# A hybrid decoder trunk on one core: six memory-key chunks opened at once, and each gated head's small products in one TensorE burst

## The chip, the cores and the metric

The kernel runs on one core of one Trainium2 chip. Its time is that of one execution on the device, in microseconds (us). Several runs are made and their median is taken. A profiled execution on the same kind of chip gives the trace from which all rows below are read; its span is counted from the first to the last instruction.

## What is computed

One decoder layer with 256 tokens and a width of 2048, all in float32, with 256 memory tokens beside it. In short:

```
memn = rms_norm(mem);  u = rms_norm(x)
proj = u @ w_in
h = x + [sigmoid(g_hg) * (hgrn2(q, f, i, og) @ w_bhg)
         + sigmoid(g_m2) * (mamba2(z, xbc, dt) @ w_bm2)] @ w_out
k, v = split(memn @ wkv)                       # 16 key chunks of 128 columns
h = h + softmax(rms_norm(h) @ wq . k) v @ wo
h = h + (gelu(conv(gate)) * up) @ w_down       # gate, up = rms_norm(h) @ w_up
out = rms_norm(h)
```

The gated branch (hgrn2) has 16 heads of 128 keys and 128 values. For each head, S_t = diag(f_t) S_{t-1} + k_t v_t^T and o_t = S_t^T q_t; then o is gated, normed over its 128 values and weighted.

## The kernel before

Activations lie transposed, features on the 128 partitions and the 256 tokens along the free axis. Each activation is held as two halves side by side, the rounded high part and the rest (512 columns, names s1 and s2), and each weight likewise as two tiles, hi and lo. A projection of one 128-column chunk is 16 products hi x [high, rest] of 512 columns (L158) followed by 16 products lo x high of 256 columns (L160), all into one bank of the pool proj. Weights arrive in float32 (1 MB a chunk, tile raw, SP's queue); ScalarE casts hi (L103) and VectorE subtracts for lo (L104), each in two pieces of 1024 columns. There are five buffers each of hi and lo, which is two and a half chunks, and the loads run two chunks ahead (AHEAD). Value projections (L188 to L190) work on tokens and take four 1 MB loads of 24 products each.

The first stage makes the 16 chunks of memory keys from s1. It opens with three chunks in step over pieces of two and then four k-blocks (L276 to L289), so that work starts before a whole chunk is there. It also makes the sums of squares of mem and x, the norms from products with ones (row_rsqrt, col_rsqrt), and s2 from x.

In the second stage three projections are made for each head, and four value loads ahead of each fourth head. The scan of a head is a Python generator, hg_scan. A list named background holds the running generators, and step(), called ahead of every weight chunk, advances each by one yield. A head's parts are: the decays (L389 to L428), the weighted decays (L430 to L437), the small products of the levels 1 to 16 into a bank of the pool lev (L445 to L455) and their masking into sm, the 32- and 64-wide blocks and the product across the two halves of the tokens into a bank of the pool misc (L466 to L476), the copies into the matrix a, the weighing of the values by a (L489, L490), and the norm (L499 and what follows). Each part comes one chunk after the one ahead of it. In the end the tile framework's scheduler decides the order on every engine, and may put one part's products among another's. Mamba's scan and the attention run as generators in the same way.

Of the kernel before, what the change touches and what calls it, by code (L numbers as in the profile page):

```python
# [19 lines left out]
P = 128  # L20
# [23 lines left out]
B = 32  # L44
MASKW = SMALL * B
# [4 lines left out]
def hybrid_trunk(ctx, tc, xT, memT, par, cst, msk, w_ka, w_va, w_hg, w_hv, w_ghg, w_bhg, w_dt,  # L50
# [102 lines left out]
    def hl_run(ps, parts, first, last):  # L153


        n = len(parts) - 1
        for i, (wh, _, hl) in enumerate(parts):
            PE.matmul(ps, lhsT=wh, rhs=hl, start=first and i == 0, stop=False)  # L158
        for i, (_, wl, hl) in enumerate(parts):
            PE.matmul(ps[:, 0:T], lhsT=wl, rhs=hl[:, 0:T], start=False, stop=last and i == n)  # L160
# [4 lines left out]
    def mm_three(ps, w, j, hl, first, last):  # L165
        wh, wl = w(j, P)
        PE.matmul(ps[:, 0:T], lhsT=wh, rhs=hl[:, 0:T], start=first, stop=False)
        PE.matmul(ps[:, 0:T], lhsT=wh, rhs=hl[:, T:2 * T], start=False, stop=False)
        PE.matmul(ps[:, 0:T], lhsT=wl, rhs=hl[:, 0:T], start=False, stop=last)
# [7 lines left out]
    def project_tok(hl):  # L177

        ps = [pj.tile([P, 512], F32, name="proj") for _ in range(2)]
        for i in range(4):  # L180
            w = weights()
            for j in range(4):
                k = 4 * i + j
                wh, wl = w(j, 512)
                for g in range(2):
                    x1 = hl[:, k, g * P:(g + 1) * P]
                    x2 = hl[:, k, T + g * P:T + (g + 1) * P]
                    PE.matmul(ps[g], lhsT=x1, rhs=wh, start=(k == 0), stop=False)  # L188
                    PE.matmul(ps[g], lhsT=x1, rhs=wl, start=False, stop=False)  # L189
                    PE.matmul(ps[g], lhsT=x2, rhs=wh, start=False, stop=(k == KD - 1))  # L190
# [75 lines left out]
    with tc.tile_pool(name="st", bufs=1) as st:  # L266
# [8 lines left out]
        nc.sync.dma_start(out=par_t[:, 0:8 * KD], in_=par[:, 0:8 * KD])  # L275
        first = [fetch(st, "raw0", 3) for _ in range(3)]  # L276
        pss = [pj.tile([P, 512], F32, name="proj") for _ in first]
        for k0, k1 in ((0, 2), (2, 4), (4, 8), (8, 12), (12, 16)):
            nc.sync.dma_start(out=mraw[:, k0:k1, :], in_=memT[:, k0:k1, :])
            for src, w in first:  # L280
                nc.sync.dma_start(out=w[0][:, P * k0:P * k1], in_=src[:, P * k0:P * k1])
            for k in range(k0, k1):
                split_scaled(s1[:, k, :], mraw[:, k, :], pc("mem_g", k))
            for (_, w), ps in zip(first, pss):
                halves(w, P * k0, P * k1)
                mm_run(ps, viewer(w[2]), [(k, s1[:, k, :]) for k in range(k0, k1)], k0 == 0,
                       k1 == KD)
            for k in range(k0, k1):
                sumsq(st, macc, mraw[:, k, :], k == 0)  # L289
        state["used"] = len(first)  # L290
        prefetch(AHEAD)

        for n in range(KD):
# [4 lines left out]
            if 3 <= n < 7:  # L298
                k = 4 * n - 12
                nc.sync.dma_start(out=xraw[:, k:k + 4, :], in_=xT[:, k:k + 4, :])  # L300
            if n == 7:
# [84 lines left out]
    def hg_scan(h, kq, zz, v):  # L386
# [18 lines left out]
        so = mp.tile([P, T], F32, name="so", bufs=2)  # L405
# [32 lines left out]
        yield True  # L438
# [507 lines left out]
```

## Time and profile before

| | us |
|---|---|
| median of 3 runs (range) | 2309.02 (2308.66 to 2310.59) |
| the profiled execution | 2308.46 |
| its span | 2306.6 |
| TensorE busy | 2285.2 (99%) |
| VectorE busy | 1579.5 (68%) |
| ScalarE busy | 1363.1 (59%) |

The busy time of an engine is a mean over stages that have different limits. A busy TensorE is not a TensorE at its peak: ends of products are modelled, so what a stretch costs is read from the starts of successive products. The granted clock is 0.999 of full speed over the span.

### The profile page before, as it was taken

To read this page: it belongs to the slowest core of one execution; us is meant where nothing else is said; L and a number is where in the kernel's file an instruction comes from. 1 tells how busy PE (TensorE), PEld (TensorE's weight loads), DVE (VectorE), ACT (ScalarE), POOL (GpSimd) and SP (SyncE) were. 2 spreads that over 40 slices of the span, in tenths; PEclk is the share of its full clock that TensorE was granted. 3 is DMA by queue.
4 is the path that set the end of the run, shared out by engine and by line. 5 is a ranking of instruction groups with operands and counts; after the bars stand their busy time and mean duration, and the time that the engine had idled before them with its cause. 6 is when DMAs were issued, how large, how long until landed. Compare 5 with 4: busy or idle time off the path is not lost.

```text
span 2306.6 us, 35693 instructions
## 1 busy us (share of the span) xinstructions
PE 2285.2 (99%) x14210; PEld 1993.5 (86%) x14210; DVE 1579.5 (68%) x2652; ACT 1363.1 (59%) x2126; POOL 1.3 (0%) x9
## 2 busy tenths in 40 slices
PE   8999999999999999999999999999999999999998
PEld 7888888888888888888888888888888888888887
DVE  8768778797555777765576765667777767755554
ACT  7566667677445778774465654556555555544443
POOL 0000000000000000000000000000000000000000
PEclk9999999999999999999999999999999999999999
DMA  8644444445555555445565644565555555556554
GB/s 288 246 171 162 158 159 163 165 161 197 183 188 187 190 192 184 173 165 192 186 242 207 224 158 171 176 217 196 184 195 188 185 196 186 187 173 198 197 196 142
DMA packets 74951, 433.92 MB, mean 188 GB/s; under 512 B 8320, under 2 KB 15904, under 8 KB 31008
## 3 DMA queue, kind: packets, MB, share of 16 engines
q1 hardware_dynamic: 74208, 430.72, 53.6%
q8 instruction: 111, 1.82, 0.3%
q10 hardware_dynamic: 576, 0.92, 0.1%
q14 instruction: 56, 0.46, 0.1%
HBM read 425.28 MB, written 6.32 MB: 187 GB/s over the span
## 4 chain that ended last, share of the span: by engine, by line
PE 94%; DVE 4%; ACT 1%; DMA 1%; issue 0%; SPq 0%; DVEq 0%
PE proj L158 54%; PE proj L160 28%; PE proj L188 3%; PE proj L189 3%; PE proj L190 3%; DVE lo L104 1%; DVE e L421 1%; PE misc L158 1%; DMA mraw<-in_memT 1%; PE lev L454 0%; DVE e L434 0%; PE misc L607 0%; PE misc L473 0%; PE misc L160 0%; PE misc L476 0%
## 5 line engine op out<-in xcount | busy, mean ns | idle before, releaser
L158 PE MATMUL proj<-s,hi 128*128 128x512 f32 x5248 | 1276.2, 393 | 8.4 <-ACT hi L103 5.7
L104 DVE TENSOR_TENSOR lo<-raw,hi 128x1024 fp32r<-128x1024 f32 (+4 forms) x827 | 937.0, 1158 | 468.3 <-PE proj L160 379.1
L158 PEld LDWEIGHTS proj<-s,hi 128*128 128x128 f32 x5248 | 962.6, 188 | 198.0 <-ACT hi L103 7.8
L103 ACT CAST hi<-raw 128x1024 fp32r<-128x1024 f32 (+4 forms) x827 | 821.6, 997 | 515.0 <-PE proj L158 410.2
L160 PEld LDWEIGHTS proj<-s,lo 128*128 128x128 f32 x5248 | 678.4, 191 | 28.2 <-DVE lo L104 0.3
L160 PE MATMUL proj<-s,lo 128*128 128x256 f32 x5248 | 688.6, 283 | 0.0
L195 ACT COPY jt<-proj 128x256 f32<-128x256 f32 x265 | 97.9, 370 | 168.5 <-PE proj L160 168.0
L188 PE MATMUL proj<-hi,s 128*128 128x512 f32 x256 | 101.0, 394 | 0.0
L190 PE MATMUL proj<-hi,s 128*128 128x512 f32 x256 | 99.8, 390 | 0.0
L189 PE MATMUL proj<-lo,s 128*128 128x512 f32 x256 | 99.7, 389 | 0.0
L789 DVE SCALAR_TENSOR_TENSOR gc<-g,par_t,gc 128x255 f32<-128x255 f32 x88 | 42.6, 484 | 54.7 <-ACT gc L787 53.1
L158 PE MATMUL proj<-ha,hi 128*128 128x512 f32 x300 | 73.7, 392 | 0.0
L158 PEld LDWEIGHTS proj<-ha,hi 128*128 128x128 f32 x300 | 54.4, 189 | 10.1
L559 DVE SCALAR_TENSOR_TENSOR sz<-t,par_t,sz 128x255 f32<-128x255 f32 (+2 forms) x96 | 46.2, 481 | 19.8 <-ACT sz L556 18.3
L190 PEld LDWEIGHTS proj<-hi,s 128*128 128x128 f32 x256 | 48.0, 188 | 10.2
L188 PEld LDWEIGHTS proj<-hi,s 128*128 128x128 f32 x256 | 48.1, 188 | 9.4
L189 PEld LDWEIGHTS proj<-lo,s 128*128 128x128 f32 x256 | 48.1, 188 | 9.3
L201 ACT COPY jt<-proj 128x256 f32<-128x256 f32 x47 | 17.5, 372 | 64.4 <-DVE h L200 46.5
L160 PEld LDWEIGHTS proj<-ha,lo 128*128 128x128 f32 x300 | 39.9, 191 | 2.3
L206 DVE SCALAR_TENSOR_TENSOR s<-h,par_t,s 128x256 fp32r<-128x256 f32 x32 | 15.5, 485 | 36.8 <-ACT s L205 36.6
L160 PE MATMUL proj<-ha,lo 128*128 128x256 f32 x300 | 40.7, 282 | 0.0
L636 ACT ACTIVATE gs<-r 128x256 f32<-128x256 f32 x32 | 13.4, 418 | 39.7 <-DVE r L196 39.7
(257 smaller groups left out, 1525.9 us busy)
## 6 DMA issues: line engine op xcount, KB each, us to landing
raw<-in_w_up SPq DMA_DIRECT2D x88, 1024.0 KB, 4.8
raw<-in_w_hg SPq DMA_DIRECT2D x48, 1024.0 KB, 4.8
raw<-in_w_m SPq DMA_DIRECT2D x48, 1024.0 KB, 4.8
raw<-in_w_dn SPq DMA_DIRECT2D x64, 704.0 KB, 4.1
raw<-in_w_hv SPq DMA_DIRECT2D x16, 1024.0 KB, 4.9
raw<-in_w_ghg SPq DMA_DIRECT2D x16, 1024.0 KB, 4.8
raw<-in_w_bhg SPq DMA_DIRECT2D x16, 1024.0 KB, 4.8
raw<-in_w_gm SPq DMA_DIRECT2D x16, 1024.0 KB, 4.8
```

The source lines that it names most:

```text
L103: S.copy(out=hi[:, c - a:d - a], in_=raw[:, c:d])
L104: V.tensor_tensor(out=lo[:, c - a:d - a], in0=raw[:, c:d], in1=hi[:, c - a:d - a].bitcast(F32), op=ALU.subtract)
L158: PE.matmul(ps, lhsT=wh, rhs=hl, start=first and i == 0, stop=False)
L160: PE.matmul(ps[:, 0:T], lhsT=wl, rhs=hl[:, 0:T], start=False, stop=last and i == n)
L188: PE.matmul(ps[g], lhsT=x1, rhs=wh, start=(k == 0), stop=False)
L189: PE.matmul(ps[g], lhsT=x1, rhs=wl, start=False, stop=False)
L190: PE.matmul(ps[g], lhsT=x2, rhs=wh, start=False, stop=(k == KD - 1))
L195: S.copy(out=tmp, in_=ps[:, T:2 * T])
L201: S.copy(out=tmp, in_=ps[:, T:2 * T])
L421: V.tensor_tensor(out=lev[hw].rearrange("p (n c i) -> p n c i", c=2, i=hw), in0=free(bb, 0, [(2 * hw, nb), (T + hw, 2), (1, hw)]), in1=fre ...
L559: V.scalar_tensor_tensor(out=o[:, s:T], in0=raw[:, 0:T - s], scalar=pc("m2_cw", 4 * c + 3 - s), in1=o[:, s:T], op0=ALU.mult, op1=ALU.add)
L789: V.scalar_tensor_tensor(out=gc[:, s:T], in0=g[:, 0:T - s], scalar=pc("f_cw", 3 * c + 2 - s), in1=gc[:, s:T], op0=ALU.mult, op1=ALU.add)
```

## The change

Three things are changed.

First, the opening. Six chunks (NS) are made at once, from a new array w_k0 in which the six chunks' columns of two k-blocks lie together. Each k-block of 768 columns is cast into one hi and one lo tile and used for all six chunks, which sum into the four banks of proj and the two of lev; the last four k-blocks are done chunk by chunk. The gains (par_t) load on ScalarE's queue, ahead of its table load, and eight products of ones with ones stand first on TensorE. The load of x, its squares and the making of s2 move to other chunks.

Second, a head's small products. The levels, the 32- and 64-wide blocks and the product across the halves are written in one part. The product across the halves has a bank of its own (ep), the wide blocks share the levels' bank, and the second 64-wide block goes to partitions 64 to 127. The next two parts come three chunks later each (pause, gap), so that in one call of step() head h-2's norm, head h-1's weighing and head h's blocks follow each other.

Third, products issued inside step() are kept in program order (mm, PIN). Everywhere else PE.matmul is only replaced by mm, which is the same instruction.

```diff
+    def mm(*args, **kwargs):
+        ins = PE.matmul(*args, **kwargs)
+        if PIN:
+            tc.keep_in_program_order(ins)
...
-    order = [w_ka[n] for n in range(KD)]
+    order = [w_ka[n] for n in range(KD - NS)]
...
     def step():
+        PIN.append(1)
         for gen in list(background):
             if next(gen, False) is False:
                 background.remove(gen)
+        PIN.pop()
...
+    def pause(n):
+        for _ in range(n):
+            yield True
...
-        nc.sync.dma_start(out=par_t[:, 0:8 * KD], in_=par[:, 0:8 * KD])
-        first = [fetch(st, "raw0", 3) for _ in range(3)]
-        pss = [pj.tile([P, 512], F32, name="proj") for _ in first]
-        for k0, k1 in ((0, 2), (2, 4), (4, 8), (8, 12), (12, 16)):
...
+        nc.scalar.dma_start(out=par_t[:, 0:8 * KD], in_=par[:, 0:8 * KD])
+        nc.scalar.preload_act_table_set("natural_log_exp_and_others")
+        wps = pm_.tile([P, 512], F32, name="misc")
+        for _ in range(8):
+            mm(wps[:, 0:P], lhsT=ones, rhs=ones, start=True, stop=True)
+        pss = [pj.tile([P, 512], F32, name="proj") for _ in range(4)] \
+            + [pl.tile([P, 512], F32, name="lev") for _ in range(NS - 4)]
+        W = NS * P
+
+        def first_block(k, raw):
+
+            split_scaled(s1[:, k, :], mraw[:, k, :], pc("mem_g", k))
+            hi = wp.tile([P, 1024], F32R, name="hi", bufs=WB)
+            lo = wp.tile([P, 1024], F32R, name="lo", bufs=WB)
+            for c, d in ((0, W // 2), (W // 2, W)) if k < 2 else ((0, W),):
+                S.copy(out=hi[:, c:d], in_=raw[:, c:d])
+                V.tensor_tensor(out=lo[:, c:d], in0=raw[:, c:d], in1=hi[:, c:d].bitcast(F32),
+                                op=ALU.subtract)
+            sumsq(st, macc, mraw[:, k, :], k == 0)
+            return hi, lo
...
+        for kk in range(KD // 2):
+            raw = st.tile([P, 2 * W], F32, name="raw0", bufs=4)
+            if kk == 0:
+                for k in range(2):
+                    nc.sync.dma_start(out=mraw[:, k, :], in_=memT[:, k, :])
+                    nc.sync.dma_start(out=raw[:, k * W:(k + 1) * W],
+                                      in_=w_k0[kk, :, k * W:(k + 1) * W])
+            else:
+                nc.sync.dma_start(out=mraw[:, 2 * kk:2 * kk + 2, :], in_=memT[:, 2 * kk:2 * kk + 2, :])
+                nc.sync.dma_start(out=raw, in_=w_k0[kk])
+            for i in range(2):
+                k = 2 * kk + i
+                parts[k] = first_block(k, raw[:, i * W:(i + 1) * W])
+                if k < KD - 4:
+                    cols = [column(n, k) for n in range(NS)]
+                    for n, (wh, _, hl) in enumerate(cols):
+                        mm(pss[n], lhsT=wh, rhs=hl, start=k == 0, stop=False)
+                    for n, (_, wl, hl) in enumerate(cols):
+                        mm(pss[n][:, 0:T], lhsT=wl, rhs=hl[:, 0:T], start=False, stop=False)
+        for n in range(NS):
+            hl_run(pss[n], [column(n, k) for k in range(KD - 4, KD)], False, True)
...
-            if 7 <= n < 15:
-                for k in (2 * n - 14, 2 * n - 13):
+            if n >= 10:
+                for k in range((n - 10) * KD // 6, (n - 9) * KD // 6):
...
-        so = mp.tile([P, T], F32, name="so", bufs=2)
+        so = mp.tile([P, T], F32, name="ho", bufs=4)
...
-        yield True
+        yield from pause(2)
...
+        ep = pl.tile([P, 512], F32, name="lev")
         W1 = B + B // 2
+        o32 = 2 * W1 + 2 * (SMALL - 1) * B
+        o64 = o32 + 2 * B
+        mm(ep[:, 0:P], lhsT=ec[:, 0:P], rhs=ec[:, P:T], start=True, stop=True)
+        for g in range(2):
+            t0 = g * P
+            mm(lp[g * 2 * B:(g + 1) * 2 * B, o64:o64 + 2 * B],
+                      lhsT=lev[64][:, t0:t0 + 2 * B], rhs=lev[64][:, t0 + 2 * B:t0 + 4 * B],
+                      start=True, stop=True)
+        for g in range(2):
+            for s0 in (0, 2 * B):
+                t0 = g * P + s0
+                mm(lp[s0:s0 + B, o32 + g * B:o32 + (g + 1) * B], lhsT=lev[32][:, t0:t0 + B],
+                          rhs=lev[32][:, t0 + B:t0 + 2 * B], start=True, stop=True)
...
+        S.copy(out=a[:, P:2 * P], in_=ep[:, 0:P])
...
-        yield True
-        ps = pm_.tile([P, 512], F32, name="misc")
+        for s0 in (0, 2 * B):
+            rows = slice(s0, s0 + B)
+            V.tensor_copy(out=free(a[rows, :], s0 + B, [(2 * P, 2), (1, B)]),
+                          in_=lp[rows, o32:o64].rearrange("p (g t) -> p g t", g=2))
         for g in range(2):
...
+            V.tensor_copy(out=a[0:2 * B, 2 * g * P + 2 * B:2 * g * P + 4 * B],
+                          in_=lp[g * 2 * B:(g + 1) * 2 * B, o64:o64 + 2 * B])
...
-        yield True
+        gap = 3 if h + 1 < HEADS else 2
+        yield from pause(gap)
...
-        yield True
+        yield from pause(gap)
```

The order of instructions shows three places. The first is the start of TensorE's program. Before, with numbers of buffers (proj_105 to proj_107 are the banks of the three chunks, hi and lo their weights):

```order
L158 MATMUL proj_105<-s1_76,hi_116 128x512 x2
L160 MATMUL proj_105<-s1_76,lo_117 128x256 x2
L158 MATMUL proj_106<-s1_76,hi_124 128x512 x2
L160 MATMUL proj_106<-s1_76,lo_125 128x256 x2
L158 MATMUL proj_107<-s1_76,hi_132 128x512 x2
L160 MATMUL proj_107<-s1_76,lo_133 128x256 x2
```

And now, where every product of TensorE has the line of mm, L66:

```order
L66 MATMUL misc_102<-ones_80 128x128 x8
L66 MATMUL proj_111<-s1_75,hi_124 128x512
L66 MATMUL proj_112<-s1_75,hi_124 128x512
L66 MATMUL proj_113<-s1_75,hi_124 128x512
L66 MATMUL proj_114<-s1_75,hi_124 128x512
L66 MATMUL lev_115<-s1_75,hi_124 128x512
L66 MATMUL lev_116<-s1_75,hi_124 128x512
L66 MATMUL proj_111<-s1_75,lo_125 128x256
```

Eight products of ones stand first, and one cast pair (hi_124, lo_125) serves six banks where three pairs served three.

The second place is a head on TensorE, in the middle of the second stage. Before (e holds the decays of the levels, ec those across the halves, a the assembled matrix, vc the values, sqs the squares for the norm):

```order
L470 MATMUL misc<-e_1727 32x32 x2
L473 MATMUL misc<-e_1727 64x64
L476 MATMUL misc<-ec 128x128
L158 MATMUL proj<-s_77,hi 128x512 x16
L160 MATMUL proj<-s_77,lo 128x256 x16
L489 MATMUL misc<-a_1170,vc 128x256
L490 MATMUL misc<-a_1170,vc 128x128
L158 MATMUL proj<-s_77,hi 128x512 x16
L160 MATMUL proj<-s_77,lo 128x256 x16
L499 MATMUL misc<-sqs,ones_r 128x256
L448 MATMUL lev<-ql,kq 32x48 x4
L454 MATMUL lev<-e_1990 32x32 x5
```

And now:

```order
L66 MATMUL proj<-s_76,lo 128x256 x16
L66 MATMUL misc<-sqs,ones_r 128x256 x2
L66 MATMUL misc<-a_1178,vc 128x256
L66 MATMUL misc<-a_1178,vc 128x128
L66 MATMUL lev<-ec 128x128
L66 MATMUL lev<-e_1992 64x64 x2
L66 MATMUL lev<-e_1992 32x32 x4
L66 MATMUL lev<-ql,kq 32x48 x4
L66 MATMUL lev<-e_1991 32x32 x12
L66 MATMUL lev<-e_1992 32x32 x4
L66 MATMUL lev<-ql,kq 32x48 x4
L66 MATMUL lev<-e_1991 32x32 x12
```

Where a group of small products stood after each projection, all of them now stand after the third.

The third place is VectorE just behind those products (sm and a take the masked blocks, lf, bb and e belong to the next head, lo is the weights' cast). Before:

```order
L463 COPY_PREDICATED sm<-msk_t,lev 128x64 x4
L479 COPY a_1170<-sm 32x2x32 x4
L104 TENSOR_TENSOR lo<-raw,hi 128x1024 x2
L196 TENSOR_TENSOR sz<-proj,jt 128x256
L482 COPY a_1170<-misc 32x2x32 x2
L484 COPY a_1170<-misc 64x2x64
L395 TENSOR_TENSOR lf<-lf,w 128x256
L402 SCALAR_TENSOR_TENSOR t<-sz,w 128x256
L396 TENSOR_TENSOR lf<-lf,w 128x256
L406 SCALAR_TENSOR_TENSOR so<-sz,w 128x256
L398 SCALAR_TENSOR_TENSOR bb<-cst_t,lf 128x256
L104 TENSOR_TENSOR lo<-raw,hi 128x1024
```

And now:

```order
L225 TENSOR_TENSOR sqs<-sq,sqs 128x256
L526 COPY_PREDICATED sm<-msk_t,lev 128x64 x2
L530 COPY a_1177<-lev 32x2x32 x2
L533 COPY a_1177<-lev 64x64 x2
L537 COPY a_1177<-sm 32x2x32 x4
L441 TENSOR_TENSOR lf<-lf,w 128x256
L448 SCALAR_TENSOR_TENSOR t<-sz,w 128x256
L442 TENSOR_TENSOR lf<-lf,w 128x256
L452 SCALAR_TENSOR_TENSOR ho<-sz,w 128x256
L444 SCALAR_TENSOR_TENSOR bb<-cst_t,lf 128x256
L112 TENSOR_TENSOR lo<-raw,hi 128x1024
L467 TENSOR_TENSOR e_2256<-bb 128x256 x3
```

Three casts stood between the masking and the decays' differences; one stands there now, behind all copies and the scan.

## Rows read from the trace of the kernel before

**Rows 1.** The page's chain that ended last, by line, share of the span

```profile
PE proj L158 54%; PE proj L160 28%; PE proj L188 3%; PE proj L189 3%; PE proj L190 3%; DVE lo L104 1%; DVE e L421 1%; PE misc L158 1%; DMA mraw<-in_memT 1%; PE lev L454 0%; DVE e L434 0%; PE misc L607 0%; PE misc L473 0%; PE misc L160 0%; PE misc L476 0%
```

**Rows 2.** Timeline, TensorE, K stage: start us, us, engine, line, operation, count

```profile
39.61 3.82 PE L158 MATMUL proj<-s,hi 128*128 128x512 f32 x16
...
45.18 3.82 PE L158 MATMUL proj<-s,hi 128*128 128x512 f32 x16
...
101.29 0.40 PE L188 MATMUL proj<-hi,s 128*128 128x512 f32 x1
...
123.08 3.79 PE L158 MATMUL proj<-s,hi 128*128 128x512 f32 x16
```

**Rows 3.** Timeline, TensorE, the opening

```profile
5.69 1.22 PE L158 MATMUL proj<-s,hi 128*128 128x512 f32 x2 [5.69 <-ACT hi L103]
...
8.41 1.05 PE L158 MATMUL proj<-s,hi 128*128 128x512 f32 x2
...
9.69 1.05 PE L158 MATMUL proj<-s,hi 128*128 128x512 f32 x2
...
10.87 0.62 PE L158 MATMUL proj<-s,hi 128*128 128x512 f32 x2
...
11.57 0.62 PE L158 MATMUL proj<-s,hi 128*128 128x512 f32 x2
...
28.86 0.67 PE L228 MATMUL misc<-macc,ones 128*128 128x256 f32 x2
...
29.73 0.48 PE L158 MATMUL proj<-s,hi 128*128 128x512 f32 x1
```

**Rows 4.** Windows: span, busy us by engine, PEclk, DMA share, GB/s

```profile
8.00:10.00 2.00, 2.00 (x8) 1.80 (x7) 1.90 (x6) 2.00 (x8) 0.00 (x0) 1.00 0.74 227
...
12.00:14.00 2.00, 0.43 (x3) 0.19 (x1) 1.70 (x5) 2.00 (x6) 0.00 (x0) 1.00 1.02 407
```

**Rows 5.** The same, four heads: PE, PEld, DVE, ACT, POOL busy

```profile
256.80:361.50 104.70, 104.22 (x880) 88.17 (x880) 84.79 (x193) 71.18 (x123) 0.00 (x0) 1.00 0.46 162
```

**Rows 6.** Timeline, TensorE, a head

```profile
200.83 0.26 PE L470 MATMUL misc<-e 128*32 128x32 f32 x4
201.01 0.33 PE L473 MATMUL misc<-e 128*64 128x64 f32 x2
...
201.71 0.49 PE L476 MATMUL misc<-ec 128*128 128x128 f32 x2
201.96 0.48 PE L188 MATMUL proj<-hi,s 128*128 128x512 f32 x1
...
207.53 0.59 PE L489 MATMUL misc<-a,vc 128*128 128x256 f32 x2
...
208.10 0.47 PE L188 MATMUL proj<-hi,s 128*128 128x512 f32 x1
...
213.65 0.40 PE L499 MATMUL misc<-sqs,ones_r 128*128 128x256 f32 x2
...
214.85 0.50 PE L188 MATMUL proj<-hi,s 128*128 128x512 f32 x1
```

**Rows 7.** Timeline, all engines, first microseconds

```profile
1.17 0.42 SPq L279 DMA_DIRECT2D mraw<-in_memT  x1
...
4.43 0.91 ACT L205 ACTIVATE s<-mraw,par_t 128x256 fp32r<-128x256 f32 x2 [1.33 <-DMA mraw<-in_memT]
```

**Rows 8.** Timeline, all engines, near the end: casts of 768 columns

```profile
2276.51 0.84 ACT L103 CAST hi<-raw 128x768 fp32r<-128x768 f32 x1 [1.70 <-PE proj L158]
...
2278.54 0.96 DVE L104 TENSOR_TENSOR lo<-raw,hi 128x768 fp32r<-128x768 f32 x1 [2.14 <-PE proj L160]
```

**Rows 9.** Timeline, TensorE, Mamba's scan: two heads on opposite partition halves

```profile
740.30 0.66 PE L607 MATMUL misc<-e,bb 128*64 128x256 f32 x4
...
741.00 0.65 PE L607 MATMUL misc<-e,bb 128*64 128x256 f32 x4
```

**Rows 10.** Windows: one head without a value load, burst to burst

```profile
299.75:319.56 19.81, 19.81 (x187) 16.61 (x181) 18.98 (x46) 14.45 (x26) 0.00 (x0) 1.00 0.47 160
```

More of the change, by code (lines that the diff above doesn't have):

```diff
@@ L44 @@
 B = 32
+NS = 6
+PIN = []
 MASKW = SMALL * B
@@ L157, in hl_run @@
         for i, (wh, _, hl) in enumerate(parts):
-            PE.matmul(ps, lhsT=wh, rhs=hl, start=first and i == 0, stop=False)
+            mm(ps, lhsT=wh, rhs=hl, start=first and i == 0, stop=False)
         for i, (_, wl, hl) in enumerate(parts):
-            PE.matmul(ps[:, 0:T], lhsT=wl, rhs=hl[:, 0:T], start=False, stop=last and i == n)
+            mm(ps[:, 0:T], lhsT=wl, rhs=hl[:, 0:T], start=False, stop=last and i == n)
     def mm_run(ps, w, items, first, last):
@@ L166, in mm_three @@
         wh, wl = w(j, P)
-        PE.matmul(ps[:, 0:T], lhsT=wh, rhs=hl[:, 0:T], start=first, stop=False)
-        PE.matmul(ps[:, 0:T], lhsT=wh, rhs=hl[:, T:2 * T], start=False, stop=False)
-        PE.matmul(ps[:, 0:T], lhsT=wl, rhs=hl[:, 0:T], start=False, stop=last)
+        mm(ps[:, 0:T], lhsT=wh, rhs=hl[:, 0:T], start=first, stop=False)
+        mm(ps[:, 0:T], lhsT=wh, rhs=hl[:, T:2 * T], start=False, stop=False)
+        mm(ps[:, 0:T], lhsT=wl, rhs=hl[:, 0:T], start=False, stop=last)
     def project(hl):
@@ L227, in row_rsqrt @@
         ps = pm_.tile([P, 512], F32, name="misc")
-        PE.matmul(ps[:, 0:T], lhsT=ones, rhs=acc, start=True, stop=True)
+        mm(ps[:, 0:T], lhsT=ones, rhs=acc, start=True, stop=True)
         rsqrt(out, ps[:, 0:T], 1.0 / D, eps_t)
@@ L234, in col_rsqrt @@
         for g in range(2):
-            PE.matmul(ps[:, g:g + 1], lhsT=acc[:, g * P:(g + 1) * P], rhs=ones[:, 0:1],
+            mm(ps[:, g:g + 1], lhsT=acc[:, g * P:(g + 1) * P], rhs=ones[:, 0:1],
                       start=True, stop=True)
@@ new lines, in column @@
+        def column(n, k):
+            c = slice(n * P, (n + 1) * P)
+            return parts[k][0][:, c], parts[k][1][:, c], s1[:, k, :]
+        parts = {}
+        for kk in range(KD // 2):
[17 more added lines that the diff above has]
+                        mm(pss[n][:, 0:T], lhsT=wl, rhs=hl[:, 0:T], start=False, stop=False)
@@ L297, in hybrid_trunk @@
                 col_rsqrt(r_mc, macc)
[L298 to L301, printed above, removed]
+            if n == 0:
+                for k in range(0, KD, 4):
+                    nc.sync.dma_start(out=xraw[:, k:k + 4, :], in_=xT[:, k:k + 4, :])
+            if n == 8:
                 nc.sync.dma_start(out=par_t[:, 8 * KD:NPAR], in_=par[:, 8 * KD:NPAR])
@@ L582, in m2_scan @@
         ps = pm_.tile([P, 512], F32, name="misc")
[L583 to L584 removed]
+        mm(ps[:, 0:T], lhsT=bm[:, 0:P], rhs=cm, start=True, stop=True)
+        mm(ps[:, T:3 * P], lhsT=bm[:, P:T], rhs=cm[:, P:T], start=True, stop=True)
         cbm = ab[g % 2]
@@ L622, in m2_scan @@
         ps = pm_.tile([P, 512], F32, name="misc")
-        PE.matmul(ps[:, 0:T], lhsT=ones, rhs=sq[:, 0, :], start=True, stop=True)
+        mm(ps[:, 0:T], lhsT=ones, rhs=sq[:, 0, :], start=True, stop=True)
         r = mp.tile([P, T], F32, name="r", bufs=1)
@@ L832, in hybrid_trunk @@
     ps = pm_.tile([P, 512], F32, name="misc")
-    PE.matmul(ps[:, 0:T], lhsT=ones, rhs=acc, start=True, stop=False)
-    PE.matmul(ps[:, 0:T], lhsT=ones, rhs=sq, start=False, stop=True)
+    mm(ps[:, 0:T], lhsT=ones, rhs=acc, start=True, stop=False)
+    mm(ps[:, 0:T], lhsT=ones, rhs=sq, start=False, stop=True)
     rsqrt(r_f, ps[:, 0:T], 1.0 / D, eps_t)
```

75 lines of the change are left out of this document (24 added, 51 removed).

## The prediction

> **What bounds the kernel now.** I read the chain of waits first. The projections' two lines on TensorE (L158, L160) hold 82% of it, the value groups' three lines 9% more [rows 1]. So only time in which TensorE does something other than a projection's product, or waits, can be won. Next came TensorE's timeline in a quiet stretch: a projection starts at 39.61 us and the next at 45.18 us, 5.57 us for 16 k-blocks, or 0.348 us a block; and the 96 products of a value group take 101.29 to 123.08 us, 21.79 us [rows 2]. With these two prices the stages can be checked for lost time, and two have some.
>
> The K stage has 16 projections, 89.1 us, and ends at 101.29 us: 12.2 us are lost. TensorE's timeline of the opening shows where [rows 3]. Nothing runs until 5.69 us. [...] The norm's products of ones take 0.87 us (28.86 to 29.73) and stay. [...]
>
> The sixteen heads repeat with a period of four. From 256.8 to 361.5 us [rows 5] TensorE needs 12 x 5.57 + 21.79 = 88.6 us for projections, and 104.7 us pass: 16.1 us per four heads go to the scans' small products and to changing over. TensorE's timeline of a head gives the prices [rows 6]: 32- and 64-wide blocks and the cross-chunk product 1.13 us (200.83 to 201.96), the weighing 0.57 us (207.53 to 208.10), the norm with the 40 small level products 1.20 us (213.65 to 214.85). Between them 24 value products take 5.57 and 5.55 us, where 24/96 of 21.79 is 5.45: a changeover costs some 0.10 to 0.12 us beyond the small products' own time. Counted in the order of instructions, TensorE leaves the projections 70 times in this stage.
>
> **The change, part by part.** *The opening.* One k-block now feeds six chunks: 6 x 0.348 = 2.09 us of TensorE. Its start: the first mraw piece is half as large and first on SP's queue. The 256 KB one was issued at 1.17 us and in use 3.3 us later [rows 7]; half of it, issued near 0.7 us, should be in use by 3.5 us. The first weights (384 KB) bring the total with par_t to 576 KB; at the 227 GB/s of 8 to 10 us [rows 4], flowing from about 2.0 us, they land at 4.6 us. A cast of half of 768 columns is half of 0.84 us [rows 8], so the first product comes near 5.1 us, 0.6 us earlier than now. After that TensorE sets the pace: a block is 512 KB, 1.3 us at the 407 GB/s seen from 12 to 14 us [rows 4], and VectorE needs 0.96 us for the cast's rest [rows 8] and some 0.9 us for the split and the norm's sum. Only blocks 1 and 2, whose data come while the queue is still slow, can be late; I take 0.8 us. [...] Lost then: 5.1 + 0.8 + 0.5 + 0.9 = 7.3 us, and 0.2 us for joins, against 12.2. **Gain 4.7 us.** [...] The joins of six chunks then fall together on ScalarE and VectorE; the next two chunks' casts have one free hi/lo pair until the fifth chunk's products end, and 1.4 us of the sixth chunk, the norm and half a projection (some 4 us) cover the second cast.
>
> *The burst.* Head h's levels, 32- and 64-wide blocks and cross-chunk product, head h-1's weighing and head h-2's norm now stand in a row: 27 changeovers instead of 70. Unchanged prices give 1.20 + 0.57 + 0.25 (201.71 to 201.96) + 0.36 for the 32-wide (two times 200.83 to 201.01) + 0.52 for the 64-wide (0.70 from 201.01 to 201.71, less 0.18) = 2.90 us a head. The two 64-wide products used to write the same partitions 0 to 63; now they write 0 to 63 and 64 to 127. The nearest row for that is Mamba's scan: two heads on opposite halves (256 + 128 columns each) take 0.70 us (740.30 to 741.00) [rows 9], where one full-width pair of the same columns takes 0.57, so two would take 1.14. By that ratio, 0.61, the 64-wide blocks cost 0.32 us and a head 2.70 us. The value lies between 0.26 and 0.52.
>
> [...] The measured 0.70 against 1.14 us speaks for overlap.
>
> Per four heads: 4 x 2.70 + 6 changeovers of 0.2 (a little more than before, since each now ends on 32-wide tiles) = 12.0 us instead of 16.1. That is 4.1 us, **16.4 us in sixteen heads.** I take off 1 us for new waits: 15.4. The bounds are 12 us (nothing overlaps, dearer changeovers) and 20 us (0.26 us and all of today's short waits gone), if VectorE keeps up.
>
> *VectorE under the burst.* All that used to be spread over a head now comes behind one burst: 6 mask operations, 8 copies, post-work of two heads, then the next head's decays; and the order shows one cast there where there were three. A head without a value group keeps VectorE busy for 18.98 of 19.81 us [rows 10], and TensorE's time for it falls to 16.7 + 2.9 = 19.6. Four heads together need 84.8 of then 100 us [rows 5], and two chunks are cast ahead (11 us). By width from the 768-column cast (0.96 us [rows 8]) a 256-column operation takes some 0.35 us, a 1024-column cast 1.3 and the small ones half of 0.35. So behind the burst VectorE has about 5 us of masks, copies and scan, a cast of 1.3, 14 operations on the decays (4.9) and another cast before the third chunk's second half is ready: 12.5 us. TensorE asks for it two chunks and a chunk's first half later, 11.1 + 4.7 = 15.8 us after the burst. So 3.3 us of cover; if it is gone, every further microsecond is TensorE's, in the twelve heads of a group's tail.
>
> *The rest at nothing.* Pinning changes the order in Mamba and attention only among the weighing's products, with the same number of changeovers. The so buffers grow from 2 to 4. x is loaded earlier, and its squares and the split of u fall into other chunks (six for u instead of eight); VectorE's sum over the K stage stays what it was. [...]
>
> Sum: 4.7 + 15.4 = 20.1 us off the profiled 2308.5 us (span 2306.6): **2288 us**. The median shown is 2309.0, half a microsecond above, which I leave in the range.
>
> **Rivals.** (a) The blocks do not overlap: 12 us from the heads, 4.7 from the opening, 2292 us. For it: separate 64-wide products cost 0.26 us each, though they stream 64 columns. (b) The opening returns nothing, because the data and the casts and not the clock set it: 2293 us. For it: SP's first weights are larger (384 against 128 KB). [...] (c) VectorE becomes the bound in the heads. Slot by slot, the chunk behind a burst holds 5 us of masks, copies and scan, 2.1 of decays, 2.6 of casts and 1.1 of joins and post-work, 10.8 us for VectorE, and TensorE takes 5.57 + 2.9 = 8.4 there. If the cover did not carry over, 2.4 us would be lost in 12 heads: 29 us, 2288 + 29 = 2317, slower than before. It turns the sign from 1.7 us a head (20.1 / 12); half of that loss gives 2302. Against it: the two other chunks of a head hold some 5.2 and 3.0 us of VectorE work in 5.57 each. (d) The change does not do what it says: a burst in program order waits for its latest input, where the scheduler now fills with products, and the waits eat the changeovers. 16 waits of 1 us leave 2304. Against: every input is made a whole head earlier.
>
> **How the numbers follow.** Forecast 0.60, its own range 2282 to 2292; (a) 0.12; (b) 0.11; (c) 0.10, of it 0.05 on the slow side; (d) 0.07, a third of it within 0.2%. What this kernel's measurement cannot tell from no change is 0.2%, 4.6 us: 2304.4 to 2313.6. Faster 0.90, same 0.04, slower 0.06. From 2282 to 2299 lie the forecast with most of its tails, (a) and (b): 0.8.
>
> **What would show it.** Right: the second projection-like run at full speed, the value group starting near 96.5 us instead of 101.3; a burst of some 2.7 us without idle time; a four-head period near 100.6 us. Wrong: TensorE waiting for lo or hi casts in the heads (c), bursts of 2.9 us or more (a), idle time inside a burst (d), a first product after 5.7 us or slow pairs beyond 8 us (b).

## The result, and the profile after

The changed kernel takes 2283.94 us (median of 4 runs, 2282.99 to 2284.70) against 2309.02: a ratio of 0.9892, 95% interval 0.9880 to 0.9905, 25.1 us less. The forecast was 2288, its range 2282 to 2299. The profiled execution took 2284.08 us (span 2282.3). The traces of all 14 kernels, this one, the one before and the twelve of the experiments, agree so well from Mamba's first burst on (1573 to 1576 us to the end of the span) that I read what a part is worth from stage boundaries: the K stage ends with the first product of the first value group, and Mamba begins with the first `misc<-sz` product, at 733.52 us before and 708.62 us after.

The chain that ended last, by line, from the page (L66 is now every product's line). As in [rows 1], it is projections and nothing else to speak of:

```profile
PE proj L66 92%; PE misc L66 2%; PE lev L66 1%; DMA xr<-in_memT 0%; DVE lo L112 0%; DMA raw<-in_w_k 0%; PE lev L71 0%; DVE s L890 0%; DVE s L220 0%; ACT L229 0%; ACT L228 0%; ACT hi L111 0%; ACT s L219 0%; DVE e L467 0%; DVE e L480 0%
```

*The opening*, TensorE's timeline of the changed kernel (start us, us, engine, line, operation, count, idle time before it and what ended it), which answers to [rows 3], and to [rows 2] by its last row:

```profile
0.99 3.78 PE L66 MATMUL misc<-ones 128*128 128x128 f32 x16 [0.99 <-POOL eps_t L264]
5.51 1.20 PE L66 MATMUL proj<-s,hi 128*128 128x512 f32 x4 [0.74 <-DVE lb L373]
...
7.72 1.08 PE L66 MATMUL proj<-s,hi 128*128 128x512 f32 x4
...
11.27 1.20 PE L66 MATMUL proj<-s,hi 128*128 128x512 f32 x4 [1.31 <-ACT hi L305]
...
40.98 0.59 PE L66 MATMUL misc<-macc,ones 128*128 128x256 f32 x2
...
97.99 0.40 PE L66 MATMUL proj<-hi,s 128*128 128x512 f32 x1
```

The first k-block of six chunks goes from 5.51 to 7.72 us: 2.21 us, at the full clock from the first product on (the trace records it, 1.00, from 5.2 us). Yet TensorE then stands still for 1.31 us. The value group starts at 97.99 us instead of 101.29, 3.3 us earlier. The windows of those microseconds (bounds, length, busy us of PE, PEld, DVE, ACT, POOL, PEclk, DMA share, GB/s) say why; they answer to [rows 4]:

```profile
3.00:5.00 2.00, 1.77 (x9) 1.47 (x7) 0.57 (x2) 0.94 (x4) 0.00 (x0) 1.00 0.98 321
...
9.00:11.00 2.00, 0.96 (x8) 0.72 (x6) 1.64 (x5) 1.61 (x4) 0.00 (x0) 1.00 1.02 417
11.00:13.00 2.00, 1.73 (x8) 1.47 (x9) 1.75 (x3) 2.00 (x6) 0.00 (x0) 1.00 1.03 423
```

The next to last column is the DMA engines' busy share: full from 3 us on, while TensorE waits. (PEclk reads 1.00 in these windows, and it reads 1.00 too from 5 to 9 us in the trace of the kernel with par_t's DMA first, further down, where the first four 512-column products take 2.08 us instead of the 1.20 above. So the level of the clock at the opening shows in the durations.)

*A burst* of the changed kernel, the same view; it answers to [rows 6]:

```profile
289.58 0.40 PE L66 MATMUL misc<-sqs,ones_r 128*128 128x256 f32 x2
289.82 0.82 PE L66 MATMUL misc<-a,vc 128*128 128x256 f32 x4
290.47 0.39 PE L66 MATMUL lev<-ec 128*128 128x128 f32 x2
290.79 0.55 PE L66 MATMUL lev<-e 128*64 128x64 f32 x9
291.14 0.23 PE L66 MATMUL lev<-ql,kq 128*32 128x48 f32 x1
...
292.05 0.50 PE L66 MATMUL proj<-hi,s 128*128 128x512 f32 x1
```

By the starts: the norm 0.24 us, the weighing 0.65, the cross-chunk product 0.32, the two 64-wide and four 32-wide blocks 0.35 (in [rows 6] they took 0.88), the 40 level products 0.91; 2.47 us with no idle time, where the prediction had 2.70. "128*64" is a product's tile, the partitions * columns of its weights (lhsT; for the 64-wide products a slice of 128 x 64); this column turns out to be the key. (A row merges products of one name in a row and shows the tile of the first: the row that starts at 290.79 us holds the two 64-wide products, the four 32-wide blocks and the first of the level products.)

Four heads and one head of the changed kernel, as windows; they answer to [rows 5] (104.70 us) and [rows 10] (19.81 us):

```profile
252.11:351.07 98.96, 98.96 (x882) 86.23 (x881) 85.36 (x197) 69.87 (x123) 0.00 (x0) 1.00 0.48 171
272.77:292.05 19.28, 19.28 (x203) 17.05 (x196) 18.48 (x47) 14.59 (x27) 0.00 (x0) 1.00 0.47 172
```

The period fell by 5.75 us. TensorE has no idle time in either window, although VectorE is busy for 18.48 of 19.28 us in the second: the cover held.

At the end of the heads something was given back. TensorE's waits over the whole run, first before (a row that the earlier section does not have), then after:

```profile
PE misc L537 <- DVE t L523: 0.4, 1, 0.4
```

```profile
PE misc L71 <- DVE t L575: 1.8, 1, 1.8
```

Both are the transposes of Mamba's time steps, one wait each; a second one, of 0.3 us (DVE ho L584), comes with it after. They need a chain of small VectorE operations, the last of which (L575) stands behind the next head's decays and a weight cast in the changed kernel's trace, from 501.07 to 504.56 us. That the burst pushed these back was not tested. From one value group to the next the heads gained 5.57, 5.75 and 5.77 us, and in the last stretch, where these waits stand, 4.51: the 21.6 us between the two marks (24.9 - 3.3).

### The profile page after: what moved, and what is told of

It is laid out like the page before. It is cut to its first block, busy times and chain, and to the rows that moved or that the text cites. A ratio compares the mean times of both kernels' runs of the same rounds, so it can differ in the third digit from the quotient of the medians.

```text
span 2282.3 us, 35723 instructions
## 1 busy us (share of the span) xinstructions
PE 2265.4 (99%) x14226; PEld 1987.0 (87%) x14226; DVE 1580.5 (69%) x2665; ACT 1358.4 (60%) x2123; POOL 1.3 (0%) x9
## 4 chain that ended last, share of the span: by engine, by line
PE 96%; DVE 2%; DMA 1%; ACT 1%; issue 0%; SPq 0%; DVEq 0%
PE proj L66 92%; PE misc L66 2%; PE lev L66 1%; DMA xr<-in_memT 0%; DVE lo L112 0%; DMA raw<-in_w_k 0%; PE lev L71 0%; DVE s L890 0%; DVE s L220 0%; ACT L229 0%; ACT L228 0%; ACT hi L111 0%; ACT s L219 0%; DVE e L467 0%; DVE e L480 0%
## 5 line engine op out<-in xcount | busy, mean ns | idle before, releaser
L66 PE MATMUL proj<-s,hi 128*128 128x512 f32 (+1 forms) x5248 | 1265.0, 391 | 3.1 <-ACT hi L305 1.3
L112 DVE TENSOR_TENSOR lo<-raw,hi 128x1024 fp32r<-128x1024 f32 (+2 forms) x806 | 920.8, 1168 | 449.1 <-PE proj L66 366.7
L66 PEld LDWEIGHTS proj<-s,hi 128*128 128x128 f32 x5248 | 961.9, 188 | 191.7 <-ACT hi L305 2.5
L111 ACT CAST hi<-raw 128x1024 fp32r<-128x1024 f32 (+2 forms) x806 | 808.0, 1006 | 508.3 <-PE proj L66 471.7
L66 PEld LDWEIGHTS proj<-s,lo 128*128 128x128 f32 x5232 | 676.4, 191 | 27.3
L66 PE MATMUL proj<-s,lo 128*128 128x256 f32 x5232 | 688.2, 283 | 0.0
L66 PE MATMUL proj<-hi,s 128*128 128x512 f32 x512 | 161.2, 391 | 0.0
L66 PEld LDWEIGHTS proj<-hi,s 128*128 128x128 f32 x512 | 95.9, 188 | 19.6
L66 PE MATMUL proj<-lo,s 128*128 128x512 f32 x256 | 99.7, 390 | 0.0
L66 PE MATMUL proj<-ha,hi 128*128 128x512 f32 (+1 forms) x340 | 80.9, 379 | 0.0
L66 PEld LDWEIGHTS proj<-ha,hi 128*128 128x128 f32 x340 | 60.7, 189 | 10.1
L66 PEld LDWEIGHTS proj<-lo,s 128*128 128x128 f32 x256 | 48.1, 188 | 9.4
L66 PE MATMUL proj<-ha,lo 128*128 128x256 f32 x320 | 46.3, 282 | 0.0
L66 PEld LDWEIGHTS proj<-ha,lo 128*128 128x128 f32 x320 | 43.8, 191 | 2.3
L480 DVE TENSOR_TENSOR e<-e,kq 128x256 f32<-128x256 f32 x96 | 34.2, 417 | 0.0
L467 DVE TENSOR_TENSOR e<-bb 128x256 f32<-128x256 f32 x96 | 33.5, 419 | 0.4
```

What stands on the lines that cost most here:

```text
L66: ins = PE.matmul(*args, **kwargs)
L111: S.copy(out=hi[:, c - a:d - a], in_=raw[:, c:d])
L112: V.tensor_tensor(out=lo[:, c - a:d - a], in0=raw[:, c:d], in1=hi[:, c - a:d - a].bitcast(F32), op=ALU.subtract)
L467: V.tensor_tensor(out=lev[hw].rearrange("p (n c i) -> p n c i", c=2, i=hw), in0=free(bb, 0, [(2 * hw, nb), (T + hw, 2), (1, hw)]), in1=fre ...
L480: V.tensor_tensor(out=ev, in0=ev, in1=free(kq, 0, [(2 * hw, nb), (T + hw, 2), (1, hw)]), op=ALU.mult)
```

## The experiments

I went in with this theory: the heads' gain is TensorE's own time (fewer changeovers, blocks side by side), the opening's comes from six chunks at once and from a clock raised by the dummies (the eight products of ones). Rivals: the delay of three chunks removed waits; the dummies do nothing; the pinning does it.

**Does it split, and do the parts add up?** Two kernels, each with one part alone.

```diff
 opening alone (hg_scan, so and the free order of before):
-        yield from pause(2)  ...  ep = pl.tile([P, 512], F32, name="lev")
+        yield True  ...           ps = pm_.tile([P, 512], F32, name="misc")
 heads alone (three chunks in step, no dummies):
-    order = [w_ka[n] for n in range(KD - NS)]
+    order = [w_ka[n] for n in range(KD)]
```

> The new opening alone (six chunks at once, dummy products, the table load on ScalarE after par_t's DMA, x loaded earlier), with the sixteen heads as in the kernel before. Theory (the opening gives what the value group's start showed, 101.29 to 97.99 us, and the rest of the gain comes from the heads): 2309.0 - 3.3 = about 2305.7 us, ratio 0.9986, and a four-head period of 104.7 us as before. Rival (part of the 21 us beyond the K stage hangs on the opening, for instance on how far ahead weights are loaded and cast): below 2303 us.

> The gated heads' burst alone, with the opening of before. Theory: the whole of the rest, 2309.0 - 21.8 = about 2287.3 us, ratio 0.9906, with a four-head period of 98.96 us as in the changed kernel; the gains of the two parts add up (3.3 + 21.8 = 25.1 us). Rival (the burst needs the new opening's state): above 2290 us.

The opening alone took 2305.11 us, ratio 0.9984 [0.9975, 0.9992], its value group starting at 98.20 us; the heads alone 2287.06, ratio 0.9906 [0.9892, 0.9919], with the period of 98.96 us. Against the kernel before as timed beside them (2308.80 us) these are 3.7 + 21.7 = 25.4, against 25.1 us: they add up, and six sevenths are the heads'.

**What in the burst is cheap: the order of the wide blocks?** The burst kept, the blocks in the old order and places:

```diff
-  ec;  64 on partitions 0-63, 64 on partitions 64-127;  32 32 32 32
+  32 32;  64 on partitions 0-63;  32 32;  64 on partitions 0-63;  ec
```

> The changed kernel, with the 32- and 64-wide blocks of a head issued in the order and on the partitions of the kernel before (two 32-wide, a 64-wide, two 32-wide, a 64-wide, both 64-wide on partitions 0 to 63), still within the burst. In the changed kernel the six take 0.35 us, in the kernel before they took 0.88. Theory (their order and places save it): 16 x 0.53 = 8.5 us slower, about 2292.5 us, and 0.8 to 0.9 us for the six in the trace. Rival (they run faster because they stand in a burst, and the gain is the changeovers'): within 1 us of 2284.

2293.63 us, ratio 0.9934 [0.9920, 0.9947]: 9.7 us slower than the changed kernel. (Its period is 2.73 us longer, 10.9 us in sixteen heads; 1.2 us come back at the transposes of the time steps, where it waits 0.6 us instead of 1.8.) The same place in this kernel's burst:

```profile
294.11 0.96 PE L66 MATMUL lev<-e 128*32 128x32 f32 x12
294.99 0.49 PE L66 MATMUL lev<-ec 128*128 128x128 f32 x2
295.41 0.29 PE L66 MATMUL lev<-ql,kq 128*32 128x48 f32 x8
```

The six blocks take 0.88 us (294.11 to 294.99), as they did in [rows 6], and the cross-chunk product, now between a 64-wide and a 32-wide product, 0.42 instead of 0.32. Standing in a burst does not make them cheap; their order or places do. Next, the order alone:

```diff
-  mm(lp[g * 2 * B:(g + 1) * 2 * B, o64:...], ...)     # 64-wide on opposite halves
+  mm(ep[0:2 * B, P + 2 * g * B:...], ...)             # both on partitions 0-63
```

> The changed kernel's order of the blocks (cross-chunk product, two 64-wide, four 32-wide, levels), but both 64-wide products on partitions 0 to 63, as in the kernel before. Writing the blocks in the old order and on the old places cost 9.6 us in sixteen heads (2293.6 against 2283.9). Theory of places (the two 64-wide products run side by side only on opposite halves, which I priced at 0.2 us a head): 16 x 0.2 = 3.2 us slower, about 2287 us, and the six blocks take 0.55 us instead of 0.35. Rival (the order alone: 64-wide and 32-wide alternating is what cost time): within 1 us of 2284, and then the 9.6 us are the order's.

2284.68 us, ratio 0.9893 [0.9878, 0.9908], not told apart from the changed kernel. In its trace:

```profile
291.84 0.66 PE L66 MATMUL lev<-e 128*64 128x64 f32 x9
292.31 0.23 PE L66 MATMUL lev<-ql,kq 128*32 128x48 f32 x1
```

0.47 instead of 0.35 us. So opposite halves save 0.12 us a head (period 99.45, 0.49 more; the edit also moves both products to the bank of the cross-chunk product), not my 0.20. In the sum most of it comes back: the transposes of the time steps wait 0.7 instead of 1.8 us. The order saves the rest, 0.41 us a head (0.88 - 0.47). Waiting for a shared place cannot be the reason: in both orders four of the six products write partitions 0 to 31, one after another, and the same six take 0.88 us in the one order and 0.47 in the other.

**Or the delay and the changeovers?** A pause of two chunks puts norm, weighing and levels behind three different chunks again:

```diff
-        gap = 3 if h + 1 < HEADS else 2
+        gap = 2
```

> The changed kernel with a pause of two chunks instead of three after a head's weighing, so that the levels, the weighing and the norm of three heads fall behind different chunks again: about 43 more changeovers. Theory of changeovers (each costs some 0.09 to 0.12 us, read from 5.57 us for 24 value products against 5.45): 4 to 5 us slower, 2288 to 2289 us. Rival (what was won is the delay: the weighing and the norm come so late that nothing is waited for, and two chunks' delay does that as well): within 1 us of 2284.

My theory falls: 2283.51 us, ratio 0.9886 [0.9870, 0.9903]. The three pieces stand alone in its trace and each costs about what it costs in the burst:

```profile
279.14 0.40 PE L66 MATMUL misc<-sqs,ones_r 128*128 128x256 f32 x2
279.38 3.82 PE L66 MATMUL proj<-s,hi 128*128 128x512 f32 x16
...
284.95 0.82 PE L66 MATMUL misc<-a,vc 128*128 128x256 f32 x4
285.52 3.92 PE L66 MATMUL proj<-s,hi 128*128 128x512 f32 x16
...
291.19 0.39 PE L66 MATMUL lev<-ec 128*128 128x128 f32 x2
```

Norm 0.24 in both, weighing 0.57 against 0.65; but the 16 products behind the weighing take 3.76 us (285.52 to 289.28) and those behind the norm 3.66, so the weighing's other 0.1 us has only moved. The period is 99.17: six more leavings of the projections cost 0.21 us, 0.035 each, where I had 0.2. (In the sum even that comes back: its transposes of the time steps wait 0.5 instead of 1.8 us.) One burst is not what was won.

**The pinning.**

```diff
-        if PIN:
-            tc.keep_in_program_order(ins)
```

> The changed kernel without the pinning of the background's products to program order; the scheduler then places them. Theory (the order is nearly the same with and without it): within 1 us of 2284. Rival (pinning is what keeps the burst in one piece): split bursts, and 2 us or more slower.

2284.83 us, ratio 0.9895 [0.9880, 0.9909], period 98.96: the bursts stay whole without it.

**A new theory: TensorE pays when the width of the tile changes.** The old order goes 128, 32, 64, 32, 64, 128; the new one 128, 64, 32. Three kernels change only the number of such steps. The first is the kernel before with its six products reordered, the second puts one 64-wide product before each pair of 32-wide ones, the third cuts each 64-wide product into two 32-wide ones:

```diff
 kernel before:   -  32 32 64 32 32 64 ec          +  ec 64 64 32 32 32 32
 changed kernel:  -  ec 64 64 32 32 32 32          +  ec 64 32 32 64 32 32
 changed kernel:  -  ec 64 64 32 32 32 32          +  ec 32 32 32 32 (64 columns each) 32 32 32 32
```

> The kernel before, with nothing changed but the order of the six block products of a head: cross-chunk product, two 64-wide, four 32-wide, on the old places and in the old slot. Theory (TensorE pays about 0.12 us each time the width of the tile changes between 128, 64 and 32; worked out from the old order costing 0.49 us a head for four more such changes): the row of changes goes from five to three, 0.24 us a head, 3.9 us in sixteen heads, about 2305 us, and the six products take about 0.9 us instead of 1.13. Rival (the old order as such costs the 9.6 us, by the 32- and 64-wide products that wait for one another): about 2300 us. Rival (it costs only inside a burst): 2309 us.

> The changed kernel with its 64-wide products on opposite halves as there, but one before each pair of 32-wide ones (64, 32, 32, 64, 32, 32). Theory of tile widths: two more changes of width, 2 x 0.12 us a head, 3.9 us slower, about 2287.8 us, and the wide blocks take 0.6 us instead of 0.35. Rival (what costs is only the old order with the cross-chunk product behind it and the shared half): within 1 us of 2284.

> The changed kernel with each 64-wide block product as two 32-wide ones (same columns streamed, four of them side by side on the four groups of 32 partitions). Theory of tile widths: the step from 128 to 64 and from 64 to 32 becomes one step from 128 to 32, 0.12 us less a head, 1.9 us faster, about 2282 us. Rival (two more weight loads and products cost as much as the step): within 0.5 us of 2284, or slower by up to 16 x 0.06 = 1 us.

The reordered old kernel took 2304.28 us, ratio 0.9979 [0.9970, 0.9987], 5.1 us faster than the kernel before as timed beside it (2309.33), by an edit that moves seven products among themselves. The alternating one took 2288.55, ratio 0.9910 [0.9896, 0.9923], 4.6 us slower than the changed kernel; the all-32-wide one 2282.81, ratio 0.9887 [0.9872, 0.9902]. All three fell where the theory had them (2305, 2287.8, 2282), though the last is not told apart from the changed kernel by time. The traces tell it. The cross-chunk product and the six blocks in the reordered kernel, then the wide blocks of the other two:

```profile
304.58 0.39 PE L467 MATMUL misc<-ec 128*128 128x128 f32 x2
304.90 0.45 PE L470 MATMUL misc<-e 128*64 128x64 f32 x4
305.28 0.32 PE L476 MATMUL misc<-e 128*32 128x32 f32 x8
305.52 0.50 PE L188 MATMUL proj<-hi,s 128*128 128x512 f32 x1
```

```profile
292.38 0.93 PE L66 MATMUL lev<-e 128*64 128x64 f32 x10
293.11 0.24 PE L66 MATMUL lev<-ql,kq 128*32 128x48 f32 x2
```

```profile
289.76 0.39 PE L66 MATMUL lev<-e 128*32 128x64 f32 x13
289.96 0.23 PE L66 MATMUL lev<-ql,kq 128*32 128x48 f32 x1
```

0.94 instead of 1.13 us; 0.73 instead of 0.35; 0.20 instead of 0.35, though that one has two products more. Counted from the traces, over four heads from one value group's first product to the next one's (the step into that product, and the leaving ahead of it, included):

| kernel | steps of width | leavings of the projections | us |
|---|---|---|---|
| before | 40 | 17 | 104.70 |
| before, reordered | 32 | 17 | 103.54 |
| changed, old blocks | 28 | 6 | 101.69 |
| changed, alternating | 20 | 6 | 100.45 |
| changed, same half | 12 | 6 | 99.45 |
| changed, three places | 12 | 12 | 99.17 |
| changed | 12 | 6 | 98.96 |
| changed, all 32 wide | 8 | 6 | 98.37 |

The windows of the six kernels of the experiments, in the table's order:

```profile
201.98:305.52 103.54, 103.10 (x885) 87.71 (x880) 84.63 (x193) 71.16 (x122) 0.00 (x0) 1.00 0.47 163
194.60:296.29 101.69, 101.69 (x888) 87.88 (x881) 84.87 (x192) 70.69 (x124) 0.00 (x0) 1.00 0.47 167
193.57:294.02 100.45, 100.45 (x887) 87.28 (x881) 85.45 (x196) 70.48 (x123) 0.00 (x0) 1.00 0.47 168
193.77:293.22 99.45, 99.45 (x888) 86.67 (x881) 84.64 (x193) 70.83 (x124) 0.00 (x0) 1.00 0.48 170
193.60:292.77 99.17, 99.17 (x887) 86.23 (x881) 85.94 (x197) 70.23 (x123) 0.00 (x0) 1.00 0.49 171
192.50:290.87 98.37, 98.37 (x904) 85.88 (x897) 84.91 (x197) 69.95 (x122) 0.00 (x0) 1.00 0.48 170
```

One step costs 1.16 / 8 = 0.145 us by the second row, (2.73 - 0.49) / 16 = 0.14 by the third (which shares the half too), 0.13 to 0.19 by the fourth (1.49 over 8, less the 0.49 if its 64-wide products, now apart, no longer run side by side), and 0.59 / 4 = 0.15 by the last. So a change of width cost 0.14 to 0.15 us in these traces. I had not weighed it.

That accounts for most of the period's 5.75 us: 28 steps fewer make 3.9 to 4.2 us, the opposite halves 0.5, 11 leavings fewer 0.4, and the two waits that the kernel before has in each period (0.26 us for `ql` and 0.22 for `sqs`, ahead of its level products) 0.5: 5.3 to 5.6. The other 0.2 to 0.5 us stay open.

**The opening: do the dummies count?**

```diff
-        for _ in range(8):
-            mm(wps[:, 0:P], lhsT=ones, rhs=ones, start=True, stop=True)
```

> The changed kernel without the eight dummy products of ones. Theory (the dummies raise the clock before the first real product): the first real products run at half speed as in the kernel before (a k-block of six chunks 4.2 us instead of 2.1), for as long as it took there, some 5 us, which costs up to 2.5 us; part of it is hidden since the data of the next blocks are late anyway (one wait of 1.31 us goes): 1.0 to 2.5 us slower, 2285 to 2286.5 us. Rival (the six chunks at once give the opening's gain and the dummies nothing): within 0.5 us of 2284.

2284.87 us, ratio 0.9897 [0.9883, 0.9910], not told apart; the value group starts at 98.18 us, 0.2 us later. TensorE's opening without the dummies, and that start:

```profile
5.54 2.08 PE L66 MATMUL proj<-s,hi 128*128 128x512 f32 x4 [5.54 <-DVE lb L370]
...
9.55 1.20 PE L66 MATMUL proj<-s,hi 128*128 128x512 f32 x4
...
11.75 1.09 PE L66 MATMUL proj<-s,hi 128*128 128x512 f32 x4
...
98.18 0.40 PE L66 MATMUL proj<-hi,s 128*128 128x512 f32 x1
```

The first k-block runs at the lower level, 4.01 us instead of 2.21, as the theory said; then nothing waits at the third, which starts 0.5 us later than with them. Most of what the clock cost, 1.8 us in the first k-block (4.01 - 2.21), the data would have cost: 0.2 us of it is left at the value group. So the opening wins 3.1 us (101.29 - 98.18) without the clock; its parts, six chunks at once and the other order of loads, were not taken apart further.

> The changed kernel with par_t's DMA first on SP's queue again, as in the kernel before, and the third and fourth k-block's weights loaded by a DMA each. In the changed kernel par_t landed at 4.06 us by ScalarE's queue, where it was in use at 2.68 us before, and the first product waited until 5.51 us; one wait of 1.31 us followed at 11.27 us for the third block's data, which come as a pair. Theory (these two waits are on the path): 1 to 2 us faster than the changed kernel, about 2282.5 us. Rival (the 16 DMA engines' rate sets the first six blocks, so a wait taken away comes back at the next block): within 0.5 us of 2284.

```diff
-        nc.scalar.dma_start(out=par_t[:, 0:8 * KD], ...)    +  nc.sync.dma_start(...)
-            if kk == 0:                                     +  if kk < 2:   # a load for each k-block
```

2282.92 us, ratio 0.9885 [0.9871, 0.9900], not told apart, the value group at 98.39 us: the rival. Its first product comes when the changed kernel's does (5.54 and 5.51 us), and it shows what I did not expect, the lower clock in spite of the dummies (4.01 us for the first k-block, 5.54 to 9.55):

```profile
0.99 3.78 PE L66 MATMUL misc<-ones 128*128 128x128 f32 x16 [0.99 <-POOL eps_t L264]
5.54 2.08 PE L66 MATMUL proj<-s,hi 128*128 128x512 f32 x4 [0.77 <-ACT hi L305]
...
9.55 1.20 PE L66 MATMUL proj<-s,hi 128*128 128x512 f32 x4
```

Ten dummies instead of eight, to close the gap ahead of the first product:

```diff
-        for _ in range(8):
+        for _ in range(10):
```

> The changed kernel with ten dummy products instead of eight, so that TensorE has no idle time between the last dummy (4.77 us with eight) and the first real product. In seven profiled executions with eight dummies the granted clock rose at 5.2, 7.1 and five times between 9.7 and 10.4 us; without dummies it rose at 9.8 us. Theory (the idle stretch of 0.4 to 1.0 us ahead of the first real product makes the rise miss): it rises by 7.2 us here. Rival (the moment of the rise is not decided by the dummies): between 9.7 and 10.4 us, with the first k-block at half speed, 4 us. The time itself stays within 1 us of 2284 either way, since the DMA engines are full from 3 to 13 us.

```profile
0.99 4.42 PE L66 MATMUL misc<-ones 128*128 128x128 f32 x20 [0.99 <-POOL eps_t L264]
5.17 1.17 PE L66 MATMUL proj<-s,hi 128*128 128x512 f32 x4
...
11.75 1.20 PE L66 MATMUL proj<-s,hi 128*128 128x512 f32 x4 [1.66 <-ACT hi L305]
```

The rise came at 5.05 us (the first moment of full clock that a trace records, which agrees with the durations), as the theory of the gap had it, but one execution decides nothing: of all nine with eight dummies it came at 4.1, 5.2, 6.3 and 7.1 us in four, each with a gap of 0.4 to 0.9 us, and late in five with gaps of 0.5 to 1.0. And it bought nothing: a wait of 1.66 us stands at the third k-block, and the value group starts at 98.28 us. (Its one time, 2286.34 us, is not compared: the granted clock is 0.50 from 507 to 510 us of its trace, 1.5 us behind the wait of 1.8 us for the time steps.)

## Why the prediction was right, and where its terms were off

The direction and the range held, and so did the place of the gain: TensorE's own time outside the projections. Its sum, 4.7 + 15.4 = 20.1 us, became 3.3 + 21.6 = 24.9. Both terms were mis-sized, the second more, and inside the second the mechanism was another. Of its 4.1 us a period 3.3 were to come from fewer changeovers (16.1 - 4 x 2.90 - 1.2); at the measured 0.035 us, 11 leavings fewer are worth 0.4. Steps of width, which the sum does not have, fell with them in the same edit and gave 3.9 to 4.2. That one stood in for the other is partly luck.

*"Per four heads: 4 x 2.70 + 6 changeovers of 0.2 = 12.0 us instead of 16.1."* It was 10.4 (98.96 - 88.6). The small products took 9.8 us and not 10.8: the 64-wide and 32-wide blocks 0.35 us and not 0.68, the cross-chunk product 0.32 and not 0.25. The rest, 0.55 us, is all that the changeovers cost, where I had 1.2. I read 0.18 us for a pair of 32-wide products and 0.26 for a 64-wide one off a slot in which they alternate [rows 6], and took them for the products' own cost; steps of width were hidden there. And I read 0.10 to 0.12 us as the price of leaving the projections. The products at the ends of those stretches are all 128 wide, so no step is in it; most of it belongs to the small products, wherever they stand: in the burst the cross-chunk product takes 0.32 us and not 0.25, the weighing 0.65 and not 0.57. The 27 changeovers for 70 were counted rightly and were nearly beside the point; what fell beside them, from 162 to 50 in the whole stage, is the steps of width, and 112 x 0.14 = 15.7 us of the gain.

*"By that ratio, 0.61, the 64-wide blocks cost 0.32 us."* Opposite halves save 0.12 us a head (0.35 against 0.47 us for the six blocks), not 0.20: the analogy to Mamba's scan [rows 9] had the sign and not the size.

*"Gain 4.7 us"* for the opening. First product 5.5 and not 5.1 us; wait 1.31 and not 0.8; the norm 0.8, nearly as priced; the x norm's 0.24 us was not in the sum; and some 1 us is left over, of which k-blocks of 2.12 us instead of 2.09 are a part. On the other side stands the clock, the 0.5 in *"Lost then: 5.1 + 0.8 + 0.5 + 0.9 = 7.3 us"*, an estimate of mine that no run shows: in the changed kernel's profiled execution the clock cost nothing, and without the dummies, where the full clock came at 9.8 us, the first k-block took 4.01 us instead of 2.21, 1.8 us more. Nor did the full clock come a fixed time after the first product: with the dummies always from 0.99 us on, it came between 4.1 and 10.4 us. That it came at 5.2 us in the changed kernel's profiled execution was luck, since in five of nine with eight dummies it came at 9.7 us or later.

*"I take off 1 us for new waits"*: 1.4 us, and the 0.3 us beside them, at the transposes of the time steps, a place that I had not named.

The rivals: (a), blocks that do not overlap, was half true (0.47 us) but lost in the order's gain. (b), an opening set by data and not the clock, was right on the mechanism and wrong on the price, since the opening wins 3.1 us without the clock. (c), VectorE as the bound: its work did not come late for the heads, only where Mamba's time steps begin beside the last of them. (d), waits in the burst, did not come: no idle time stands in a burst.

No kernel here is shown to beat the changed one. The best candidate is the all-32-wide one, 1.9 us earlier at Mamba's start by the trace (706.71 us) and 1.1 us by its median, inside the intervals. Its transposes of the time steps wait 2.3 us; with a pause of two chunks, as in the three-places kernel (0.5 us), about 1 us of that might stay won after the four extra 0.21 us; that was not tried.

## What to carry to other kernels

Before pricing small products off a trace, look at the tile beside each row and count how often its width changes: group products by width, end a group on the width that comes next, and try a 64-wide product as two 32-wide ones if its neighbours are 32 wide (0.59 us in four heads by the trace here; the kernel's time does not tell it apart). Where a product stood among the projections mattered little here (0.035 us a leaving); what it stood next to did (0.14 to 0.15 us a step of width). The faster clock at the start was worth only what the first loads left of it, 0.2 of 1.8 us, so look at the DMA share of those microseconds first (0.98 to 1.03 from 3 us on here).

## What the runs showed of the hardware that was not expected

- A step between tile widths of 128, 64 and 32 cost 0.14 to 0.15 us (1.16 us for 8 steps, 0.59 for 4); leaving the projections for a product of the same width and coming back cost 0.035 us (0.21 for 6).
- The moment at which the full clock was granted was not tied to the first product. With dummies from 0.99 us on it came, in ten executions of kernels with this opening, at 4.1, 5.05, 5.2, 6.3, 7.1 and five times between 9.7 and 10.4 us; without dummies at 9.8, and in three with the old opening, where products start at 5.7 to 7.1 us, at 10.0 to 10.7. The end of the K stage, 97.3 to 98.4 us, follows it by half a microsecond only: 97.8 us on the mean of the five early ones, 98.3 of the five late ones.
- The clock fell in a busy stretch (with ten dummies TensorE was busy for 3.00 of 3.00 us from 507 to 510 us, at a PEclk of 0.50). In 2 of the 7 traces that wait 1.8 us or more for the time steps it was granted at 0.50 for 3.4 us, from 506.8 us (ten dummies) and 508.3 us (heads alone), 1.5 and 0.8 us after the wait's end.
